# Three-pass matmul products over pairs of accumulators, and a third weight staging buffer, in a convolution and attention trunk step

## The chip, the cores and the metric

The kernel runs on one core of one Trainium2 chip. The metric is the device time of one execution in microseconds (us). In the shares and tables, PE is the matmul engine, PEld its weight loads, DVE the vector engine, ACT the scalar engine, POOL the GpSimd engine, and SP the engine that issues nearly all of the loads and stores.

## The reference

The reference computes one inference step of a trunk with two layers, D = 1024, in float32. The first layer is a convolution module and a SwiGLU feed-forward part (FFN). The second is chunked attention on one shared K/V and a second FFN. Cut to what this case touches:

```python
def swiglu_ffn(h, g, w_in, w_out):
    a, b = jnp.split(rms_norm(h, g) @ w_in, 2, axis=-1)
    return h + (jax.nn.silu(a) * b) @ w_out

def conv_module(h, hist, g, w_pw1, b_pw1, w_dw, b_dw, ln_g, ln_b, w_pw2, b_pw2):
    a, gate = jnp.split(rms_norm(h, g) @ w_pw1 + b_pw1, 2, axis=-1)
    glu = a * jax.nn.sigmoid(gate)
    full = jnp.concatenate([hist.astype(glu.dtype), glu], axis=1)
    y = lax.conv_general_dilated(full, w_dw[:, None, :], window_strides=(1,), padding="VALID", ...) + b_dw
    y = jax.nn.silu(layer_norm(y, ln_g, ln_b))
    return h + y @ w_pw2 + b_pw2, full[:, -CONV_HIST:]
```

There are 512 prompt tokens (one stream) and 128 sample tokens (8 streams of 16). The convolution is causal, one filter of width 31 for each channel. The FFN has 2816 hidden channels.

## The kernel before

**Data.** Activations lie with channels on the 128 partitions and tokens along the free axis, 8 channel tiles of 128. The 640 tokens are two groups: group 0 has 256 columns (the samples and the first prompt tokens), group 1 has 384.

**Products.** A float32 product is made of three products of rounded parts. Each operand is split into a high part, which is rounded, and a low part, the rest. `mm3` (L169) fills one accumulator in PSUM: for each of the 8 channel tiles k it issues high weights with high values (L172), low weights with high values (L173) and high weights with low values (L174), one behind the other. The pool `mm` has four accumulators.

**Weights.** `wsplit` (L130) brings a weight tile of 128 x 2048 into SBUF and splits it: SP loads `raw` (L141, or L136 for the second FFN product), ACT copies it to `whi` (L152), and `wlo = raw - whi` is made by DVE and POOL together (L156): POOL takes the last `pool` quarters of the columns, DVE the first ones. `raw`, `whi` and `wlo` have two buffers each in the pool `wp`. Such a tile serves two output tiles of 8 channel tiles, a first half and a second half.

**Stages.** The string `PLAN` sets in which order the early work is written; a scheduler, which runs on a timeline model, then sets the order in which each engine's queue holds it. In the convolution module `glu` (L371) multiplies with `in_w_pw` and gates; `conv` (L422) filters channel tiles on DVE, one instruction per filter tap into PSUM (L439); `conv_pool` filters others on ACT and POOL (L419); `conv_pe` filters others by matmuls (L471), whose operand goes from SBUF to DRAM (`sc`, L454) and back in shifted copies (`x`, L457). `conv_ln` (L476) makes the layer norm: sums of channel tiles on POOL (`acc`, L197), a matmul with ones (L206), one that spreads the result over the partitions (L218), y minus the mean, squares on ACT (L181) and their sums on POOL (L197), again L206 and L218, the product with the reciprocal deviation (L491), the activation (L493), and the split into high and low parts called z in the code and `x` in the profile (L161 on ACT, L162 on DVE). `pw2` (L498) multiplies z with the second pointwise weights: in group 1 two weight tiles at a time are in work. The FFN of group 0 (`ffn_in` L273, `out_tile` L298, `ffn_out` L307) is written between the convolution and the layer norm of group 1, so that PE has work while DVE filters group 1. In `ffn_in` each weight tile gives the two halves a and b of a hidden tile; silu(a)·b becomes `hid` (ACT L289, DVE L290), which is split as well (L161, L162). Behind `pw2` of group 1 stands the rest of the FFN, then attention, then the second FFN, whose matmuls are written elsewhere (L971).

Of the kernel before, what the change touches and what calls it, by code (L numbers as in the profile page):

```python
# [8 lines left out]
F32 = mybir.dt.float32  # L9
F32R = mybir.dt.float32r  # L10
AF = mybir.ActivationFunctionType
ALU = mybir.AluOpType
PSUM = bass.MemoryType.PSUM

P = 128
# [64 lines left out]
def tile_trunk(ctx, tc, xT, vecs, hist, w_pw1, w_pw2, w_in0, w_out0, w_in1, w_out1,  # L80
# [7 lines left out]

    uid = [0]
# [40 lines left out]
    def wsplit(src, k, n, parts=1, pool=0, cuts=1, gains=None):  # L130
        raw = wp.tile([P, 2048], F32, tag="raw", name=nm("raw"))
# [37 lines left out]
    def mm3(ps, wts, xs):  # L169
        last = len(wts) - 1  # L170
        for i, ((wh, wl), (xh, xl)) in enumerate(zip(wts, xs)):
            nc.tensor.matmul(ps, wh, xh, start=(i == 0), stop=False)  # L172
            nc.tensor.matmul(ps, wl, xh, start=False, stop=False)  # L173
            nc.tensor.matmul(ps, wh, xl, start=False, stop=(i == last))  # L174

# [97 lines left out]
    def ffn_in(wsrc, j, xs, hid, jj, groups, pool):  # L273
        wh, wl = wsplit(wsrc[j], 16, P, pool=pool)
        for g in groups:
            n = GR[g][1]
            ps = []
            for ab in range(2):
                pt = mmt()
                mm3(pt[:, :n], [(wh[:, (ab * 8 + k) * P:(ab * 8 + k + 1) * P],  # L280
                                 wl[:, (ab * 8 + k) * P:(ab * 8 + k + 1) * P]) for k in range(KT)],
                    xk(xs[g], range(KT)))
                ps.append(pt[:, :n])
# [14 lines left out]
    def out_tile(wts, ch, b, m, g, hid):  # L298
        wh, wl = wts
        n = GR[g][1]  # L300
        pt = mmt()
        mm3(pt[:, :n], [(wh[:, (b + k) * P:(b + k + 1) * P], wl[:, (b + k) * P:(b + k + 1) * P])
                        for k in range(ch)], xk(hid[g], range(ch)))
        with tc.high_priority(offset=HP):
            nc.vector.tensor_tensor(out=hp(g, m), in0=pt[:, :n], in1=hp(g, m), op=ALU.add)

    def ffn_out(wsrc, j0, ch, hid, groups, pool):  # L307
        mg = 4 if ch <= 4 else 2 if ch <= 8 else 1
        ws = []
        for m0 in range(0, KT, mg):  # L310
            src = wsrc[m0:m0 + mg, :, j0 * P:(j0 + ch) * P].rearrange("m p c -> p m c")
            ws.append(wsplit(src, ch * mg, P, parts=mg, pool=pool))
            if mg == 4:
                continue
            for m in range(m0, m0 + mg):
                for g in groups:
                    out_tile(ws[-1], ch, (m - m0) * ch, m, g, hid)
        if mg == 4:
            for g in groups:
                for m in range(KT):  # L320
                    out_tile(ws[m // mg], ch, (m % mg) * ch, m, g, hid)
# [49 lines left out]
    def glu(c, g, wh, wl):  # L371
        n = GR[g][1]
        ps = []
        for ab in range(2):
            pt = mmt()
            mm3(pt[:, :n], [(wh[:, (ab * 8 + k) * P:(ab * 8 + k + 1) * P],
                             wl[:, (ab * 8 + k) * P:(ab * 8 + k + 1) * P]) for k in range(KT)],
                xk(xs[g], range(KT)))
            ps.append(pt[:, :n])
# [118 lines left out]
    def pw2(g, z):  # L498
        n = GR[g][1]
        for m2 in range(KT // 2):  # L500
            wh, wl = wsplit(w_pw2[m2], 16, P, pool=PL2[g])
            for i in range(2):
                m = 2 * m2 + i
                pt = mmt()
                mm3(pt[:, :n], [(wh[:, (i * 8 + k) * P:(i * 8 + k + 1) * P],
                                 wl[:, (i * 8 + k) * P:(i * 8 + k + 1) * P]) for k in range(KT)],
                    xk(z, range(KT)))
                nc.vector.scalar_tensor_tensor(out=hp(g, m), in0=pt[:, :n], scalar=col(V_BPW2, m),
                                               in1=hp(g, m), op0=ALU.add, op1=ALU.add)
# [56 lines left out]
    hid0.close()  # L566

# [740 lines left out]
```

## Time and profile before

| | |
|---|---|
| time, median of 3 runs | 1544.46 us (1542.37 to 1546.8) |
| profiled execution: time | 1545.65 us |
| profiled execution: span | 1543.9 us |
| mean granted TensorE clock | 0.988 of full speed |
| instructions | 27207 |
| HBM read, written | 187.55 MB, 11.22 MB |
| matmul records of L172, L173, L174 from x (1344 each) | 412.5, 415.9, 411.9 us busy |
| the same from hid (352 each) | 104.4, 107.7, 105.9 us busy |
| whi (117 copies on ACT, L152) | 197.8 us busy, mean 1694 ns |

A row of a group of instructions gives the line, the engine, the operation, output and inputs by the program's names, the shapes, the count, then busy time and mean duration. A row of waits names who waited, "<-", for whom, then us in total, how often and the longest. A row of stretches gives start and end, the length, then for each engine its busy us (with its number of instructions), the granted clock, the share of the DMA engines and what they moved. A row of the timeline gives start, duration (of all merged instructions), the instruction, and in brackets the idle time before it and who ended it. The lines themselves stand in the prediction.

### The profile page before, as it was taken

Reading aid. Unit: us, or ns where it says so; the run is one execution under the profiler, and the core shown is the slowest. Engines: PE = TensorE matmul, PEld = TensorE weight load, DVE = VectorE, ACT = ScalarE, POOL = GpSimd, SP = SyncE. Lnnn points to the kernel's source line nnn. Section 1 sums busy time; section 2 is a strip of 40 time slices with the busy share of each in tenths; the row PEclk is TensorE's granted clock in tenths of the full one; section 3 lists DMA queues with packets and bytes.
Section 4 is the critical chain, followed back from the end, with each engine's and each line's share of the span. In section 5 each row is a group of like instructions: output and inputs, shape, how many; then the busy total and the mean of one; then the engine's idle time right before and its main releaser. Section 6 shows DMA issues by size and latency. Waiting matters only on the chain.

```text
span 1543.9 us, 27207 instructions
## 1 busy us (share of the span) xinstructions
PE 1470.9 (95%) x11054; PEld 1397.5 (91%) x11054; DVE 1041.2 (67%) x1890; ACT 666.6 (43%) x1196; POOL 450.6 (29%) x406
## 2 busy tenths in 40 slices
PE   5888998989999999999999999998999999999998
PEld 5878888988999999999988798886989999999998
DVE  6894999988545445456566767666797466467456
ACT  4544454535433323235455445443564144244244
POOL 6965468977501000001322111110421011011010
PEclk9999999999999999999999999998999999999999
DMA  7784335445421333433555545444003222222222
GB/s 232 240 228 143 138 113 164 144 156 164 137 83 56 130 116 130 133 118 124 194 180 196 182 143 200 150 153 140 28 28 116 76 83 89 76 83 89 76 83 83
DMA packets 57022, 200.54 MB, mean 130 GB/s; under 512 B 10176, under 2 KB 20672, under 8 KB 44096
## 3 DMA queue, kind: packets, MB, share of 16 engines
q1 hardware_dynamic: 56608, 198.48, 39.1%
q8 instruction: 87, 1.43, 0.4%
q10 hardware_dynamic: 288, 0.31, 0.1%
q14 instruction: 39, 0.32, 0.1%
HBM read 187.55 MB, written 11.22 MB: 129 GB/s over the span
## 4 chain that ended last, share of the span: by engine, by line
PE 71%; DVE 15%; DMA 4%; issue 4%; ACT 3%; POOL 3%; SPq 0%; POOLq 0%; ACTq 0%; DVEq 0%
PE mm L172 13%; PE mm L174 13%; PE mm L173 13%; PE pb L971 6%; DVE w L439 5%; PE pc L971 4%; PE pa L971 3%; DVE wlo L156 3%; PE w L797 1%; PE pb L172 1%; DMA raw<-in_w_pw 1%; PE pb L173 1%; PE pb L174 1%; PE pa L174 1%; PE pa L172 1%
## 5 line engine op out<-in xcount | busy, mean ns | idle before, releaser
L173 PE MATMUL mm<-x,wlo 128*128 128x256 f32 (+1 forms) x1344 | 415.9, 311 | 15.0 <-DVE wlo L156 14.1
L172 PE MATMUL mm<-x,whi 128*128 128x256 f32 (+1 forms) x1344 | 412.5, 311 | 6.1 <-ACT x L161 3.7
L174 PE MATMUL mm<-x,whi 128*128 128x256 f32 (+1 forms) x1344 | 411.9, 310 | 0.6 <-DVE x L162 0.3
L152 ACT ACTIVATE whi<-raw 128x2048 fp32r<-128x2048 f32 (+2 forms) x117 | 197.8, 1694 | 228.5 <-PE mm L174 138.0
L173 PEld LDWEIGHTS mm<-x,wlo 128*128 128x128 f32 x1344 | 255.7, 190 | 18.7 <-DVE wlo L156 17.0
L172 PEld LDWEIGHTS mm<-x,whi 128*128 128x128 f32 x1344 | 253.4, 190 | 11.3 <-ACT x L161 4.1
L174 PEld LDWEIGHTS mm<-x,whi 128*128 128x128 f32 x1344 | 254.0, 190 | 3.0 <-DVE x L162 1.9
L156 DVE TENSOR_TENSOR wlo<-raw,whi 128x2048 fp32r<-128x2048 f32 (+5 forms) x117 | 207.8, 1779 | 63.3 <-ACT whi L152 59.5
L156 POOL TENSOR_TENSOR wlo<-raw,whi 128x1536 fp32r<-128x1536 f32 (+3 forms) x50 | 146.5, 2932 | 66.8 <-ACT whi L152 66.5
L916 POOL TENSOR_TENSOR raw<-raw 128x512 f32<-128x512 f32 x38 | 56.4, 1485 | 327.0 <-DVE raw L916 262.9
L173 PE MATMUL mm<-hid,wlo 128*128 128x256 f32 (+1 forms) x352 | 107.7, 309 | 6.7 <-DVE wlo L156 6.7
L174 PE MATMUL mm<-hid,whi 128*128 128x256 f32 (+1 forms) x352 | 105.9, 307 | 0.8 <-DVE hid L162 0.7
L439 DVE SCALAR_TENSOR_TENSOR w<-gp,dwv,w 128x384 f32<-128x384 f32 x180 | 103.9, 612 | 0.8
L172 PE MATMUL mm<-hid,whi 128*128 128x256 f32 (+1 forms) x352 | 104.4, 307 | 0.0
L197 POOL TENSOR_TENSOR acc<-sq,sq 128x384 f32<-128x384 f32 (+1 forms) x8 | 8.0, 1004 | 259.6 <-ACT sq L181 259.5
L173 PEld LDWEIGHTS mm<-hid,wlo 128*128 128x128 f32 x352 | 66.1, 188 | 7.9 <-DVE wlo L156 7.9
L419 POOL TENSOR_TENSOR y<-y,cvt 128x256 f32<-128x256 f32 (+1 forms) x60 | 67.0, 1117 | 4.6 <-ACT cvt L418 2.2
L174 PEld LDWEIGHTS mm<-hid,whi 128*128 128x128 f32 x352 | 65.8, 188 | 1.2 <-DVE hid L162 1.2
L172 PEld LDWEIGHTS mm<-hid,whi 128*128 128x128 f32 x352 | 65.1, 188 | 0.2
L161 ACT ACTIVATE whi<-raw 128x1024 fp32r<-128x1024 f32 x38 | 39.4, 1054 | 54.7 <-DVE raw L916 19.1
L971 PE MATMUL pa<-x0f,whi 128*128 128x320 f32 x228 | 60.1, 311 | 2.7 <-DVE t L916 1.2
L197 POOL TENSOR_TENSOR acc<-acc,sq 128x384 f32<-128x384 f32 (+1 forms) x48 | 52.6, 1096 | 29.1 <-ACT sq L181 27.7
(326 smaller groups left out, 3496.6 us busy)
## 6 DMA issues: line engine op xcount, KB each, us to landing
raw<-in_w_in SPq DMA_DIRECT2D x62, 1024.0 KB
raw<-in_w_out SPq DMA_DIRECT2D x36, 768.0 KB
raw<-in_w_pw SPq DMA_DIRECT2D x22, 1024.0 KB
cache<-in_ck SPq DMA_DIRECT2D x32, 512.0 KB
cache<-in_cv SPq DMA_DIRECT2D x32, 512.0 KB
raw<-in_w_kq SPq DMA_DIRECT2D x8, 1024.0 KB
x<-sc SPq DMA_DIRECT2D x16, 368.0 KB
raw<-in_w_out SPq DMA_DIRECT2D x4, 1024.0 KB
```

Of the source, the lines that this page charges most:

```text
L152: nc.scalar.activation(out=hi[:, a:b], in_=raw[:, a:b], func=AF.Copy)
L156: eng.tensor_tensor(out=lo[:, a:b], in0=raw[:, a:b], in1=hi[:, a:b].bitcast(F32), op=ALU.subtract)
L161: nc.scalar.activation(out=hi, in_=src, func=AF.Copy)
L172: nc.tensor.matmul(ps, wh, xh, start=(i == 0), stop=False)
L173: nc.tensor.matmul(ps, wl, xh, start=False, stop=False)
L174: nc.tensor.matmul(ps, wh, xl, start=False, stop=(i == last))
L197: last["acc"] = eng.tensor_tensor(out=acc[:, :n], in0=prev, in1=s(), op=ALU.add)
L419: nc.gpsimd.tensor_tensor(out=y[g][:, c, :], in0=y[g][:, c, :], in1=pr[:, :n], op=ALU.add)
L439: nc.vector.scalar_tensor_tensor(out=dst, in0=src, scalar=wj, in1=dst, op0=ALU.mult, op1=ALU.add)
L797: nc.tensor.matmul(st[32 * b:32 * b + 32, 0:512], qv[b], KC[b // 2][:, b % 2, :], start=True, stop=True)
L916: ENG[e].tensor_tensor(out=out, in0=a, in1=b, op=op)
L971: nc.tensor.matmul(ps, a[:, c], b[:, k, :], start=(first and k == 0 and i == 0), stop=(k == 3 and i == 2), skip_group_check=not first)
```

## The change

A pool `rx` with one buffer is opened beside `wp`. Every third call of `wsplit` takes its `raw` from there, until the pool is closed ahead of attention; there are then three raw buffers in turn, while `whi` and `wlo` keep two each. A new function `mm3s` fills several accumulators together in three passes over all channel tiles: high with high, high weights with low values, low weights with high values; within a pass it goes through k, and at each k through the accumulators. `glu`, `ffn_in` and `pw2` give it the pair of output tiles of one weight tile, and `out_tile` becomes `out_tiles`, which takes pairs too (`ffn_out` then loops over groups outside the pair). Both accumulators of a pair are finished at its end, one matmul apart. The number of matmuls, vector, scalar and GpSimd instructions and loads stays what it was. Where attention and the second FFN use their own products, nothing is written anew, and PE's order there is unchanged.

```diff
+    rxs = ExitStack()
+    third = [0, rxs.enter_context(tc.tile_pool(name="rx", bufs=1, side="right"))]
...
     def wsplit(src, k, n, parts=1, pool=0, cuts=1, gains=None):
-        raw = wp.tile([P, 2048], F32, tag="raw", name=nm("raw"))
+        third[0] += 1
+        pool3, tag = (third[1], "rx") if third[1] and third[0] % 3 == 0 else (wp, "raw")
+        raw = pool3.tile([P, 2048], F32, tag=tag, name=nm(tag))
...
+    def mm3s(pss, wtss, xs):
+        n = len(xs) - 1
+        for step in range(3):
+            for i, (xh, xl) in enumerate(xs):
+                for ps, wts in zip(pss, wtss):
+                    wh, wl = wts[i]
+                    nc.tensor.matmul(ps, (wh, wh, wl)[step], (xh, xl, xh)[step],
+                                     start=(step == 0 and i == 0), stop=(step == 2 and i == n))
...
-            ps = []
-            for ab in range(2):
-                pt = mmt()
-                mm3(pt[:, :n], [(wh[:, (ab * 8 + k) * P:(ab * 8 + k + 1) * P],
-                                 wl[:, (ab * 8 + k) * P:(ab * 8 + k + 1) * P]) for k in range(KT)],
-                    xk(xs[g], range(KT)))
-                ps.append(pt[:, :n])
+            ps = [mmt()[:, :n] for _ in range(2)]
+            mm3s(ps, [[(wh[:, (ab * 8 + k) * P:(ab * 8 + k + 1) * P],
+                        wl[:, (ab * 8 + k) * P:(ab * 8 + k + 1) * P]) for k in range(KT)]
+                      for ab in range(2)], xk(xs[g], range(KT)))
...
-            for m in range(m0, m0 + mg):
-                for g in groups:
-                    out_tile(ws[-1], ch, (m - m0) * ch, m, g, hid)
+            for g in groups:
+                out_tiles(ws[-1], ch, range(0, mg * ch, ch), range(m0, m0 + mg), g, hid)
...
     ffn({1: hp1}, w_in0, w_out0, {1: xs1}, (1,), FD)
     hid1.close()
     hid0.close()
+    rxs.close()
+    third[1] = None
```

The scheduler sets the queues anew. The order is shown at three places; names end in the program's running number, which differs by a few between the two programs, and line numbers are 4 to 10 higher in the changed one.

**DVE, in the first FFN of group 0, beside the taps of group 1.** `t` is silu(a)·b of a hidden tile, `hid` its low part, `w_...` an accumulator of the taps in PSUM. Before:

```order
L290 TENSOR_TENSOR t_301_2409<-t_300_2408,mm_2383 128x256
L439 SCALAR_TENSOR_TENSOR w_366_2820<-gp,dwv,w_366_2820 128x384
L439 SCALAR_TENSOR_TENSOR w_367_2885<-gp,dwv,w_367_2885 128x384
L439 SCALAR_TENSOR_TENSOR w_366_2820<-gp,dwv,w_366_2820 128x384
L156 TENSOR_TENSOR wlo_2479<-raw_2477,whi_2478 128x512
L162 TENSOR_TENSOR hid_2161<-t_301_2409,hid_2161 128x256
```

Now:

```order
L160 TENSOR_TENSOR wlo_2482<-raw_2480,whi_2481 128x512
L447 SCALAR_TENSOR_TENSOR w_367_2888<-gp,dwv,w_367_2888 128x384
L300 TENSOR_TENSOR t_301_2412<-t_300_2411,mm_2362 128x256
L447 SCALAR_TENSOR_TENSOR w_366_2823<-gp,dwv,w_366_2823 128x384
L447 SCALAR_TENSOR_TENSOR w_367_2888<-gp,dwv,w_367_2888 128x384
L166 TENSOR_TENSOR hid_2164<-t_301_2412,hid_2164 128x256
```

The low weights have moved from a place behind t and three taps to a place ahead of t; t and hid have two taps between them where the low weights and three taps stood. Ahead of the last tap DVE holds 479 instructions before and 477 now.

**PE, the start of `pw2` in group 1.** `x_3013` (now `x_3016`) is z of group 1; an `Activation` wait is for a high part (of z, or of the weights), a `DVE` wait for a low part or for an accumulator. Before:

```order
L172 MATMUL mm_4195<-x_3013,whi_4189 128x384 [waits Activation_49]
L172 MATMUL mm_4221<-x_3013,whi_4189 128x384 [waits DVE_49]
L173 MATMUL mm_4195<-x_3013,wlo_4190 128x384 [waits DVE_49]
L174 MATMUL mm_4195<-x_3013,whi_4189 128x384
L172 MATMUL mm_4195<-x_3013,whi_4189 128x384
L173 MATMUL mm_4195<-x_3013,wlo_4190 128x384
```

Now:

```order
L186 MATMUL mm_4198<-x_3016,whi_4192 128x384 [waits DVE_49,Activation_49]
L186 MATMUL mm_4198<-x_3016,whi_4192 128x384 [waits Activation_49]
L186 MATMUL mm_4199<-x_3016,whi_4192 128x384 [waits DVE_49]
L186 MATMUL mm_4199<-x_3016,whi_4192 128x384
L186 MATMUL mm_4257<-x_3016,whi_4251 128x384 [waits DVE_49,Activation_49]
L186 MATMUL mm_4257<-x_3016,whi_4251 128x384
L186 MATMUL mm_4258<-x_3016,whi_4251 128x384 [waits DVE_49]
L186 MATMUL mm_4258<-x_3016,whi_4251 128x384
L186 MATMUL mm_4198<-x_3016,whi_4192 128x384 [waits Activation_49]
```

Before, the products of k stand in threes, and those of the last k come near the end of the 96 matmuls of the four accumulators. Now the 32 products of high parts of all four accumulators stand first, the last k of z from the 29th on, and then all with low values, and all with low weights.

**SP, the loads of the early convolution.** `raw` and `rx` are weight tiles of 1.0 MB; `sc` and `x` are the way through DRAM of `conv_pe`. Before:

```order
L141 DMA raw_599<-in_w_pw 128x2048
L141 DMA raw_666<-in_w_pw 128x2048
L454 DMA sc_735<-gs 128x740
L141 DMA raw_883<-in_w_pw 128x2048
L457 DMA x_94_737<-sc_735 32x4x736 x4
L141 DMA raw_950<-in_w_pw 128x2048
L454 DMA sc_778<-gs 128x740
L141 DMA raw_1045<-in_w_pw 128x2048
L457 DMA x_98_780<-sc_778 32x4x736 x4
L141 DMA raw_1158<-in_w_pw 128x2048
L543 DMA out_convs<-gs 1024x1x368
L454 DMA sc_1108<-gs 128x740
```

Now:

```order
L145 DMA raw_669<-in_w_pw 128x2048
L145 DMA raw_886<-in_w_pw 128x2048
L145 DMA rx_953<-in_w_pw 128x2048
L462 DMA sc_738<-gs 128x740
L465 DMA x_94_740<-sc_738 32x4x736 x4
L145 DMA raw_1048<-in_w_pw 128x2048
L145 DMA raw_1161<-in_w_pw 128x2048
L462 DMA sc_781<-gs 128x740
L145 DMA rx_1447<-in_w_pw 128x2048
L465 DMA x_98_783<-sc_781 32x4x736 x4
L145 DMA raw_1509<-in_w_pw 128x2048
L551 DMA out_convs<-gs 1024x1x368
```

One or two more weight tiles now stand ahead of each `sc`: `raw_886` and `rx_953` ahead of the first, and `rx_1447` and `raw_1509` ahead of the third, which followed it before.

More of the change, by code (lines that the diff above doesn't have):

```diff
@@ L296, in ffn_in, with out_tiles @@
                 xsplit(t[:, :n], hid[g][0][:, jj, :], hid[g][1][:, jj, :])
-    def out_tile(wts, ch, b, m, g, hid):
+    def out_tiles(wts, ch, bs, ms, g, hid):
         wh, wl = wts
         n = GR[g][1]
[L301 to L305, printed above, removed]
+        ps = [mmt()[:, :n] for _ in ms]
+        mm3s(ps, [[(wh[:, (b + k) * P:(b + k + 1) * P], wl[:, (b + k) * P:(b + k + 1) * P])
+                   for k in range(ch)] for b in bs], xk(hid[g], range(ch)))
+        for m, pt in zip(ms, ps):
+            with tc.high_priority(offset=HP):
+                nc.vector.tensor_tensor(out=hp(g, m), in0=pt, in1=hp(g, m), op=ALU.add)
     def ffn_out(wsrc, j0, ch, hid, groups, pool):
@@ L314, in ffn_out @@
                 continue
-            for m in range(m0, m0 + mg):
-                for g in groups:
-                    out_tile(ws[-1], ch, (m - m0) * ch, m, g, hid)
+            for g in groups:
+                out_tiles(ws[-1], ch, range(0, mg * ch, ch), range(m0, m0 + mg), g, hid)
         if mg == 4:
             for g in groups:
-                for m in range(KT):
-                    out_tile(ws[m // mg], ch, (m % mg) * ch, m, g, hid)
+                for m in range(0, KT, 2):
+                    out_tiles(ws[m // mg], ch, ((m % mg) * ch, (m % mg + 1) * ch), (m, m + 1), g,
+                              hid)
     def ffn(pool, w_in, w_out, xs, groups, chunks, pl=0, og=None, cm=CM, pad=(0, 0)):
@@ L372, in glu @@
         n = GR[g][1]
[L373 to L379, printed above, removed]
+        ps = [mmt()[:, :n] for _ in range(2)]
+        mm3s(ps, [[(wh[:, (ab * 8 + k) * P:(ab * 8 + k + 1) * P],
+                    wl[:, (ab * 8 + k) * P:(ab * 8 + k + 1) * P]) for k in range(KT)]
+                  for ab in range(2)], xk(xs[g], range(KT)))
         with tc.high_priority(offset=HP):
@@ L501, in pw2 @@
             wh, wl = wsplit(w_pw2[m2], 16, P, pool=PL2[g])
-            for i in range(2):
-                m = 2 * m2 + i
[L504 to L508, printed above, removed]
+            ps = [mmt()[:, :n] for _ in range(2)]
+            mm3s(ps, [[(wh[:, (i * 8 + k) * P:(i * 8 + k + 1) * P],
+                        wl[:, (i * 8 + k) * P:(i * 8 + k + 1) * P]) for k in range(KT)]
+                      for i in range(2)], xk(z, range(KT)))
+            for i, pt in enumerate(ps):
+                m = 2 * m2 + i
+                nc.vector.scalar_tensor_tensor(out=hp(g, m), in0=pt, scalar=col(V_BPW2, m),
                                                in1=hp(g, m), op0=ALU.add, op1=ALU.add)
```

## The prediction

> **What bounds the kernel now.** I read the page first, then all engines by stretches of the span.
>
> ```profile
> PE 1470.9 (95%) x11054; PEld 1397.5 (91%) x11054; DVE 1041.2 (67%) x1890; ACT 666.6 (43%) x1196; POOL 450.6 (29%) x406
> ...
> 80.00:120.00 40.00, 34.68 (x290) 28.54 (x292) 35.50 (x71) 16.90 (x27) 21.84 (x21) 0.91 0.83 236
> 150.00:200.00 50.00, 44.91 (x341) 40.43 (x342) 48.71 (x80) 24.25 (x37) 24.19 (x14) 0.93 0.37 129
> 200.00:250.00 50.00, 45.06 (x359) 43.13 (x358) 50.00 (x88) 27.32 (x42) 38.95 (x20) 1.00 0.37 115
> 250.00:300.00 50.00, 44.75 (x373) 43.55 (x374) 50.00 (x84) 26.69 (x34) 45.34 (x23) 1.00 0.51 173
> 395.00:450.00 55.00, 55.00 (x357) 55.00 (x356) 27.67 (x43) 21.88 (x33) 17.29 (x10) 1.00 0.33 114
> 600.00:720.00 120.00, 120.00 (x694) 120.00 (x694) 62.14 (x73) 40.02 (x44) 2.26 (x3) 1.00 0.37 123
> ```
>
> PE is busy for 95% of the span. It has no idle time at all from 395 on, where the first FFN of group 1 runs (the last two rows are the two ends of it). So what the change gives must come from ahead of 395. There the limit differs. From 150 to 300 DVE is full (48.71, 50.00 and 50.00 of 50 us), while PE has some 5 us idle in each 50: PE waits for what DVE makes. Now the waits of PE: first the whole span, then 150 to 300, then 300 to 400.
>
> ```profile
> PE mm L173 <- DVE wlo L156: 20.8, 18, 3.6
> PE mm L471 <- DMA x<-sc: 8.4, 2, 4.6
> ...
> PE mm L172 <- ACT whi L152: 1.2, 2, 1.0
> ...
> PE mm L173 <- DVE wlo L156: 11.5, 13, 2.4
> ...
> PE mm L173 <- DVE wlo L156: 9.3, 5, 3.6
> ```
>
> The three passes aim at the wait for low weights. It is 20.8 us in all, 11.5 of it where DVE is full and 9.3 behind that. These are the most that the edit can take away directly.
>
> **The change, part by part. Matmuls.** Their number and shapes stay. New is that PE changes its accumulator at every matmul.
>
> ```profile
> 288.98 0.28 PE L172 MATMUL mm<-x,whi 128*128 128x256 f32 x1
> 289.10 0.28 PE L173 MATMUL mm<-x,wlo 128*128 128x256 f32 x1
> ...
> 598.78 0.34 PE L173 MATMUL mm<-x,wlo 128*128 128x384 f32 x1
> 598.95 0.34 PE L174 MATMUL mm<-x,whi 128*128 128x384 f32 x1
> ...
> 1250.73 0.31 PE L971 MATMUL pa<-x0f,whi 128*128 128x320 f32 x1
> 1250.88 1.92 PE L971 MATMUL pb<-xe,bk 128*128 128x320 f32 x12
> ```
>
> Starts are 0.12 us apart with 256 columns and 0.17 with 384. In the second FFN a change from accumulator `pa` to `pb` costs no more than its 320 columns, 0.15. I take the alternation at nothing. Bounds: a hundredth either way of the some 720 us where it is used would be 7 us, but the rows give no reason for either sign.
>
> **Stretch 0 to 154.** Two tiles wait there for their high weights (1.2 us in the waits above), which an earlier load can take away. Against that, one or two more weight tiles stand on SP ahead of the convolution's way through DRAM. Its worst case now is on the chain:
>
> ```profile
> 81.08 9.73 DMA sc<-gs
> ...
> 102.58 6.49 PE L471 MATMUL mm<-x,w 128*32 128x256 f32 x64 [4.64 <-DMA x<-sc]
> ```
>
> A tile of 1.05 MB at the 236 GB/s of the row 80 to 120 is 4.4 us. Queued ahead of `sc` it delays that matmul by up to this; the PE work moved in front can win back as much. Bounds −4.4 and +4.4 (for the first of the two loads the same tiles were already nearly through), I take −0.5.
>
> **Stretch 150 to 338.** Here DVE sets the pace, and the change takes nothing from it: as many low weights, taps and splits stand ahead of the last tap (477 instructions for 479). PE now asks for the low weights only at its 33rd matmul of a tile, 32 x 0.12 = 3.8 us later. That hides a wait of 0.3 to 2.4 us once; but a PE that runs ahead of a full DVE waits for the next thing it makes (`hid`, a freed accumulator). So of the 11.5 us I count nothing for the last tap. What DVE's own instructions cost is open:
>
> ```profile
> L439 DVE SCALAR_TENSOR_TENSOR w<-gp,dwv,w 128x384 f32<-128x384 f32 x180 | 103.9, 612 | 0.8
> L156 DVE TENSOR_TENSOR wlo<-raw,whi 128x512 fp32r<-128x512 f32 x13 | 23.5, 1806 | 0.0
> ...
> L162 DVE TENSOR_TENSOR hid<-t,hid 128x256 fp32r<-128x256 f32 x12 | 10.0, 833 | 0.0
> ...
> 322.81 3.56 DVE L156 TENSOR_TENSOR wlo<-raw,whi 128x512 fp32r<-128x512 f32 x1
> 335.67 0.69 DVE L156 TENSOR_TENSOR wlo<-raw,whi 128x512 fp32r<-128x512 f32 x1 [1.51 <-ACT whi L152]
> 336.27 3.71 DVE L162 TENSOR_TENSOR hid<-t,hid 128x256 fp32r<-128x256 f32 x1
> ...
> 335.71 3.99 POOL L156 TENSOR_TENSOR wlo<-raw,whi 128x1536 fp32r<-128x1536 f32 x1 [2.42 <-ACT whi L152]
> ```
>
> (The first three rows are the groups of 154 to 328.) The same 512 columns took 0.69 us and 3.56; the `hid` of 256 columns took 3.71 while POOL's share of the low weights ran from 335.71 to 339.70, and ended as that ended. The taps, whose long operand lies in PSUM and not in SBUF, keep to 0.6. So a DVE instruction with both inputs in SBUF can be held up by POOL's. The changed order sets low weights, t and hid differently against POOL's part; the mean of 1.81 may go to 0.69 or to 3.56. I take no change, and price the two sides as rivals below. The Trainium skill, page "SBUF — State Buffer", section "Who interferes with whom", states this as a rule: such an instruction shares a read port with GpSimd, and who issues first blocks the other for the whole instruction; by that rule the cost hangs on who comes first, which the new order may settle either way. The rows agree (3.71 beside POOL's 3.99, 0.69 just ahead of it).
>
> **Layer norm of group 1.**
>
> ```profile
> 327.15 1.26 DVE L439 SCALAR_TENSOR_TENSOR w<-gp,dwv,w 128x384 f32<-128x384 f32 x2
> ...
> 329.65 3.64 POOL L197 TENSOR_TENSOR acc<-acc,y 128x384 f32<-128x384 f32 x3
> ...
> 307.57 0.38 PE L173 MATMUL mm<-hid,wlo 128*128 128x256 f32 x1 [1.38 <-DVE wlo L156]
> 313.95 0.39 PE L173 MATMUL mm<-hid,wlo 128*128 128x256 f32 x1 [1.68 <-DVE wlo L156]
> 326.42 0.39 PE L173 MATMUL mm<-x,wlo 128*128 128x256 f32 x1 [3.56 <-DVE wlo L156]
> 338.65 0.72 PE L206 MATMUL w<-onec,acc 128*128 128x1 f32 x6
> ...
> 324.00:328.00 4.00, 1.58 (x9) 1.58 (x10) 3.96 (x5) 0.80 (x1) 4.00 (x2) 0.85 0.23 31
> 328.00:332.00 4.00, 4.00 (x27) 4.00 (x27) 2.24 (x2) 1.25 (x3) 3.92 (x3) 0.72 0.81 264
> ```
>
> The last tap ends at 328.4, POOL's sums at 333.3, yet PE's L206 that reads them comes at 338.65: here PE is late by 5.4 us, since 1.38 + 1.68 + 3.56 = 6.6 us of waits lie ahead, and behind the longest of them the granted clock was 0.85 and 0.72 (0.15 x 1.6 + 0.28 x 4 = 1.4 us). If these 8.0 us go, and PE still has 24 matmuls more ahead of L206 than before (24 x 0.12 = 2.9), L206 comes 5.1 us earlier, just behind the sums. Bounds 0 and 5.4; I take 4, as PE then waits more for DVE. The Trainium skill, page "TensorE: Matmul & The Clock Gate", section "HAM oscillation — how this bites in real kernels", puts the limit at a gap of some 3.4 us, behind which the clock halves; by it the term for the clock would be half of 3.4, 1.7 us in place of 1.4. The trace agrees: the gap of 3.56 was followed by 0.72.
>
> **`pw2` of group 1** takes part of this back.
>
> ```profile
> 368.97 0.72 PE L206 MATMUL w<-onec,acc 128*128 128x1 f32 x6
> ...
> 381.24 6.54 DMA raw<-in_w_pw
> ...
> 389.83 1.23 DVE L156 TENSOR_TENSOR wlo<-raw,whi 128x1024 fp32r<-128x1024 f32 x1 [2.05 <-ACT whi L152]
> ...
> 394.98 0.92 ACT L161 ACTIVATE x<-n 128x384 fp32r<-128x384 f32 x2
> ...
> 403.15 0.51 PE L172 MATMUL mm<-x,whi 128*128 128x384 f32 x2
> ```
>
> L206 at 368.97 follows POOL's second sums, so the 4 us hold up to z. The load of 6.54 us, on the chain now, starts sooner through the third buffer, which also takes DVE's idle 2.05 us for its low weights away. The last high part of z, at 394.98 + 0.92 = 395.9 now, so comes at 395.9 − 4 − 2.05 = 389.8. But the three passes need all eight high parts within the first 32 of the 96 matmuls of four accumulators: behind the last part stand 4 + 64 = 68 matmuls, 68 x 0.173 = 11.8 us, so they end at 401.6. Before they end at about 403.2, as the last part was needed only near the end (403.15 is the first row behind them). Gain 1.6 us; with 5.4 for 4 it is 3.0; with nothing saved ahead of z the last part comes at 393.9 and they end at 405.7, 2.5 later than now. I take a gain of 2.5: ACT too gives z's last parts sooner when its copies of weights no longer fall between them.
>
> **From 395 on** nothing: PE is full and its order from attention on is the old one. The waits for low weights that the passes would hide there are none: the row from 395 to 450 has 55.00 of 55.
>
> **The sum** against the profiled execution: 1545.65 − 0.5 − 2.5 = 1542.65. That execution lies 1.2 above the median of 1544.46, so the forecast is 1.8 under the median. About 0.3%, 4.6 us, is what a measurement tells from no change: 1539.8 to 1549.1 count as same.
>
> **Rivals.** (B) *The waits really go and DVE gets faster.* If the low weights' 13 instructions of 512 columns fall from 1.81 us to near the 0.69, DVE's stretch is shorter by up to 13 x 1.1 = 14.5 us, and the last tap with it. For it: DVE is full there, and each us passes to the last tap. Against: the same two engines split the same tiles at the same signal, whi. With two thirds of it, 9.7, and the sum's 3.0: 1533; with all of the 14.5, 1528.
>
> (C) *Slower: DVE is held up more.* Place: DVE's low weights and `hid` in 150 to 328. Price: the 12 rows of `hid` at a mean of 0.83 us reach 3.71 when they fall into POOL's 3.99; the hid split now stands some 2.5 us (wlo, tap, t, two taps) behind the low weights that start with POOL's part, so still within it. If a third of the 12 is hit more, 4 x 2.9 = 11.5 us later, less the sum's 3: 1545.65 + 11.5 − 3 = 1554; with a quarter 1551. It decides from a hold-up of 1549.1 − 1542.65 = 6.5 us on, where the time leaves the same.
>
> (D) *The loads behind more weight tiles.* The two waits of 8.4 us on `x<-sc` grow by up to 4.4: 1542.65 + 4.9 = 1547.5. For: SP is one queue, and the row 80 to 120 has the DMA engines 83% busy. Against: the extra tile is wanted anyway, and its later place is then free.
>
> (E) *The change does not do what it says:* with two buffers for whi and wlo still, a third raw tile only waits longer for its split, and z's end eats what the passes win. Then 1545.65.
>
> **How the numbers follow.** Forecast 0.47, of which 0.10 falls under 1539.8 and 0.37 within same (its own range 1538 to 1547); B 0.25, all faster; C 0.15, slower; D 0.08, of which 0.02 slower; E 0.05, same. Faster 0.10 + 0.25 = 0.35; same 0.37 + 0.06 + 0.05 = 0.48; slower 0.15 + 0.02 = 0.17. The range leaves out about a third of B at the bottom and of C at the top: 1530 to 1552.
>
> **What would show it.** Right: PE's wait for low weights falls from 20.8 to under 3, but DVE stays full from 150 to 300 and the last tap stays within 3 us of 328.4; PE's L206 comes at 333 to 336 in place of 338.65; PE then waits inside the first 32 matmuls of `pw2` for high parts of z; from there on both traces run in parallel, some 3 us apart. Wrong: a last tap at 318 or earlier (B) or at 333 and later (C), with the mean of low weights on DVE moved from 1.81; a wait on `x<-sc` above 8.4 in all (D); or a pitch other than 0.12 and 0.17 in dense stretches.

## The result, and the profile after

| | median | range | runs |
|---|---|---|---|
| before | 1545.39 us | 1542.37 to 1546.80 | 4 |
| changed | 1568.65 us | 1567.57 to 1569.97 | 4 |

The changed kernel is slower: ratio 1.0158, 95% interval 1.0140 to 1.0177. The profiled execution of the changed kernel has a span of 1565.9 us (1543.9 before), 22.0 more. First its engines and its stretches (the same cuts as before, columns as in the table of before), then what PE waits for over the whole span, and at last PE's waits from 0 to 150 alone.

```profile
PE 1481.7 (95%) x11054; PEld 1409.6 (90%) x11054; DVE 1045.9 (67%) x1890; ACT 668.8 (43%) x1196; POOL 448.4 (29%) x406
...
80.00:120.00 40.00, 34.98 (x270) 29.42 (x268) 33.88 (x69) 17.11 (x29) 24.24 (x23) 0.91 0.78 221
150.00:200.00 50.00, 42.28 (x320) 38.08 (x318) 45.91 (x74) 24.25 (x36) 25.62 (x16) 0.86 0.32 107
200.00:250.00 50.00, 40.58 (x293) 38.67 (x290) 49.29 (x74) 23.51 (x37) 28.01 (x16) 0.93 0.33 96
250.00:300.00 50.00, 43.61 (x336) 42.81 (x335) 49.06 (x79) 22.25 (x28) 41.12 (x22) 0.90 0.47 158
300.00:340.00 40.00, 33.34 (x260) 32.54 (x259) 37.40 (x61) 17.75 (x25) 30.19 (x17) 0.91 0.36 110
395.00:450.00 55.00, 51.27 (x317) 50.86 (x317) 32.74 (x48) 27.28 (x38) 22.18 (x13) 0.94 0.43 149
500.00:600.00 100.00, 100.00 (x608) 99.98 (x607) 50.84 (x69) 32.42 (x42) 6.06 (x8) 1.00 0.32 107
```

```profile
PE mm L186 <- DVE t L300: 16.5, 9, 2.4
PE mm L186 <- ACT x L165: 11.7, 8, 3.3
PE mm L479 <- ACT t L393: 5.4, 2, 4.8
PE mm L479 <- DMA x<-sc: 4.7, 1, 4.7
PE w L231 <- POOL rst L245: 3.9, 2, 2.7
PE mm L186 <- DVE h L316: 3.7, 1, 3.7
...
PE mm L186 <- DVE wlo L160: 0.2, 1, 0.2
...
PE mm L186 <- ACT x L165: 2.7, 3, 1.5
```

The reader is to see three things. The wait for low weights, 20.8 us before, is down to 0.2: the change does what it is built for. In its place stand 16.5 us for `t` (silu(a)·b, whose making frees the second accumulator of a pair) and 11.7 us for high parts of x. And PE, with the same 11054 matmuls, is busy for 1481.7 us where it was 1470.9: idle time makes 84.2 − 73.0 = 11.2 of the 22.0 us, and slower matmuls the other 10.8, as the granted clock of 150 to 340 shows (0.86 to 0.93; before 0.93 to 1.00).

When the same work is reached in the two profiled executions, in us from the span's start:

| place | before | changed | later by |
|---|---|---|---|
| second sums of group 0's layer norm (PE L206, ahead of z) | 148.8 | 152.9 | 4.1 |
| first high part of x of group 0, for the FFN (ACT) | 197.4 | 206.0 | 8.6 |
| last one, end | 205.8 | 219.9 | 14.1 |
| t of the first hidden tile (DVE) | 215.1 | 231.7 | 16.6 |
| t of the sixth | 246.2 | 263.8 | 17.6 |
| last tap, end | 328.4 | 347.0 | 18.6 |
| first sums of group 1's layer norm (PE L206) | 338.65 | 358.02 | 19.4 |
| first sum h of `pw2` in group 1 (DVE) | 398.5 | 419.0 | 20.5 |
| last sum of the first FFN | 730.4 | 754.3 | 23.9 |

So nearly all is lost by the last tap, and the largest piece, 12.5 of it, between 153 and 232. Of these 12.5 us 4.5 are lost up to the first high part of x, while `pw2` of group 0 is multiplied (the granted clock of 150 to 200 is 0.86, 0.93 before), and 8.0 behind it, where x of group 0 is normalised and the first two hidden tiles are multiplied. Here is that second part in the timeline of the changed kernel, DVE, POOL, ACT and PE one behind the other:

```profile
195.34 3.42 DVE L160 TENSOR_TENSOR wlo<-rx,whi 128x512 fp32r<-128x512 f32 x1
211.84 3.14 DVE L166 TENSOR_TENSOR x<-n,x 128x256 fp32r<-128x256 f32 x1
215.77 0.68 DVE L160 TENSOR_TENSOR wlo<-raw,whi 128x512 fp32r<-128x512 f32 x1
...
194.72 3.49 POOL L160 TENSOR_TENSOR wlo<-rx,whi 128x1536 fp32r<-128x1536 f32 x1 [2.35 <-PE mm L186]
211.23 3.47 POOL L160 TENSOR_TENSOR wlo<-raw,whi 128x1536 fp32r<-128x1536 f32 x1 [10.84 <-ACT whi L156]
...
219.49 0.40 ACT L165 ACTIVATE x<-n 128x256 fp32r<-128x256 f32 x1
...
217.34 1.22 PE L186 MATMUL mm<-x,whi 128*128 128x256 f32 x4 [3.33 <-ACT x L165]
219.95 5.17 PE L186 MATMUL mm<-x,whi 128*128 128x256 f32 x31 [1.39 <-ACT x L165]
```

One low part of x, 0.42 us elsewhere, takes 3.14 while POOL splits the weights of the second hidden tile, and that tile's `wlo` of DVE stands in the queue ahead of the last two parts of x. PE stops for the seventh and for the eighth high part, as its first pass asks for all of them.

### The profile page after: what moved, and what is told of

The parts are those of the page before. It is cut to its first block, busy times and chain, and to the rows that moved or that the text cites. A ratio compares the mean times of both kernels' runs of the same rounds, so it can differ in the third digit from the quotient of the medians.

```text
span 1565.9 us, 27254 instructions
## 1 busy us (share of the span) xinstructions
PE 1481.7 (95%) x11054; PEld 1409.6 (90%) x11054; DVE 1045.9 (67%) x1890; ACT 668.8 (43%) x1196; POOL 448.4 (29%) x406
## 4 chain that ended last, share of the span: by engine, by line
PE 70%; DVE 13%; ACT 3%; issue 2%; POOL 1%; DMA 1%; POOLq 0%; DVEq 0%; ACTq 0%
PE mm L186 25%; PE pb L981 6%; PE mm L176 4%; PE pc L981 4%; PE mm L177 4%; PE mm L178 4%; DVE wlo L160 4%; PE pa L981 4%; DVE w L447 3%; ACT whi L156 1%; PE pb L176 1%; PE pb L177 1%; PE pb L178 1%; PE w L807 1%; PE pa L178 1%
## 5 line engine op out<-in xcount | busy, mean ns | idle before, releaser
L186 PE MATMUL mm<-x,whi 128*128 128x384 f32 (+1 forms) x2176 | 347.5, 317 | 25.7 <-ACT x L165 11.7
L186 PEld LDWEIGHTS mm<-x,whi 128*128 128x128 f32 x2176 | 332.9, 196 | 32.3 <-ACT x L165 13.8
L156 ACT ACTIVATE whi<-raw 128x2048 fp32r<-128x2048 f32 (+2 forms) x87 | 143.7, 1657 | 158.3 <-PE mm L186 94.4
L186 PE MATMUL mm<-x,wlo 128*128 128x384 f32 (+1 forms) x1088 | 169.9, 308 | 0.2 <-DVE wlo L160 0.2
L186 PEld LDWEIGHTS mm<-x,wlo 128*128 128x128 f32 x1088 | 161.0, 188 | 0.3 <-DVE wlo L160 0.3
L186 PE MATMUL mm<-hid,whi 128*128 128x256 f32 (+1 forms) x704 | 113.7, 316 | 8.4 <-DVE t L300 6.3
L186 PEld LDWEIGHTS mm<-hid,whi 128*128 128x128 f32 x704 | 107.4, 196 | 10.3 <-DVE t L300 6.9
L160 POOL TENSOR_TENSOR wlo<-raw,whi 128x1536 fp32r<-128x1536 f32 (+3 forms) x33 | 89.8, 2726 | 64.5 <-ACT whi L156 45.6
L176 PE MATMUL mm<-x,whi 128*128 128x256 f32 (+1 forms) x256 | 80.5, 315 | 1.1 <-DVE h L316 1.1
L177 PE MATMUL mm<-x,wlo 128*128 128x256 f32 (+1 forms) x256 | 79.9, 312 | 0.0
L178 PE MATMUL mm<-x,whi 128*128 128x256 f32 (+1 forms) x256 | 79.5, 310 | 0.0
L160 DVE TENSOR_TENSOR wlo<-rx,whi 128x2048 fp32r<-128x2048 f32 (+4 forms) x30 | 60.2, 2006 | 9.2 <-ACT whi L156 9.2
```

The costliest lines, as they stand in the source:

```text
L156: nc.scalar.activation(out=hi[:, a:b], in_=raw[:, a:b], func=AF.Copy)
L160: eng.tensor_tensor(out=lo[:, a:b], in0=raw[:, a:b], in1=hi[:, a:b].bitcast(F32), op=ALU.subtract)
L186: nc.tensor.matmul(ps, (wh, wh, wl)[step], (xh, xl, xh)[step], start=(step == 0 and i == 0), stop=(step == 2 and i == n))
```

## The experiments

Each kernel was run beside the kernel before on the same chip; a ratio is to that kernel, with its 95% interval. Times in us are medians.

### Which half of the change

Third buffer alone (`wsplit` as in the change, `mm3` as before):

```diff
-        raw = wp.tile([P, 2048], F32, tag="raw", name=nm("raw"))
+        third[0] += 1
+        pool3, tag = (third[1], "rx") if third[1] and third[0] % 3 == 0 else (wp, "raw")
+        raw = pool3.tile([P, 2048], F32, tag=tag, name=nm(tag))
```

> The third staging buffer alone, products as before the change. Theory R (the third buffer puts weight tiles ahead of the convolution's loads, and that is what the 23 us are): about 1555 to 1568 us, and the waits on x<-sc above the 8.4 us of before. Theory X (the first pass needs all eight high parts of x at once) and theory P (both accumulators of a pair must be free at its first matmuls, and are released only at its end): within 5 us of before, 1540 to 1550, with some 20 us of waits for low weights as before.

Measured: 1541.37, ratio 0.9979 (0.9966 to 0.9992). Three passes alone, two raw buffers:

```diff
-    third = [0, rxs.enter_context(tc.tile_pool(name="rx", bufs=1, side="right"))]
+    third = [0, None]
```

> The three passes over pairs as in the change, but two staging buffers as before it. R: near the time before, 1545 to 1552. X and P: nearly all of the loss stays, 1561 to 1570, with waits of PE for the high parts of x and for t (silu(a)*b, which frees the second accumulator) of 10 us and more each.

Measured: 1571.12, ratio 1.0162 (1.0128 to 1.0196). So the third buffer is not the cause, and all of the loss comes with the passes over pairs. Without the third buffer the waits on `x<-sc` were 15.0 us, so the delay of the early convolution is not owed to it either: the scheduler sets SP's queue anew for every variant. The 0.2% of the third buffer alone are not located: at the last sum of the first FFN that profiled execution is 1.3 us behind the one before, and its gain lies behind that, in attention and the second FFN, which the buffer doesn't touch.

### What in the passes: the pair, or the order within it

One accumulator after the other, each in three passes:

```diff
-        for step in range(3):
-            for i, (xh, xl) in enumerate(xs):
-                for ps, wts in zip(pss, wtss):
+        for ps, wts in zip(pss, wtss):
+            for step in range(3):
+                for i, (xh, xl) in enumerate(xs):
```

> As the change, but the three passes run over one accumulator, then over the other of the pair; so the first is released half a tile earlier, and the second is needed half a tile later. P: the waits for t fall from 16.5 us to under 4 and the time by some 8 to 14 us, to 1555 to 1561. X: the high parts of x are needed even sooner (8 matmuls), those waits stay at 10 us or more, and the time stays at 1563 to 1570.

Measured: 1560.59, ratio 1.0101 (1.0071 to 1.0131). The waits for t fell to 5.1 us, near what theory P expected, though 16.3 us of waits on `x<-sc` came up. Pairs, but by channel tile:

```diff
-        for step in range(3):
-            for i, (xh, xl) in enumerate(xs):
+        for i, (xh, xl) in enumerate(xs):
+            for step in (0, 2, 1):
```

> As the change, but within a pair all three products of a channel tile k stand together, so that high parts of x are needed one by one as before the change; both accumulators are still filled together. X: the waits for high parts of x fall from 11.7 us to under 4, and the time by 8 to 14 us, to 1555 to 1561. P: the waits for t stay near 16 us and the time at 1563 to 1570. Waits for low weights come back under both, as they are needed at the third matmul or so.

Measured: 1549.76, ratio 1.0024 (1.0008 to 1.0039), better than theory X expected. PE's waits in this kernel:

```profile
PE mm L186 <- DVE wlo L160: 23.1, 19, 3.8
PE w L219 <- DVE acc L210: 12.8, 1, 12.8
PE mm L186 <- ACT x L165: 6.3, 2, 5.3
...
PE mm L176 <- DVE h L316: 2.5, 1, 2.5
```

The pairs are still there, but the waits for `t` of a hidden tile are gone from the list and the old wait for low weights is back, 23.1 us of it, and the kernel is 19 us faster than the changed one. So theory P as I put it falls too: a pair held to its end does not by itself make PE wait for t; only with low weights out of the way does PE come early enough for that. The pairs do cost something, 0.45% against the third buffer alone (1.0024 and 0.9979, with intervals that don't overlap). The larger piece, 1.34% between 1.0024 and 1.0158, hangs on the order of the products within the pair. A milder form of the passes, one accumulator at a time, with the low weights behind all the rest:

```diff
+    def mm3w(ps, wts, xs):
+        last = len(wts) - 1
+        for i, ((wh, wl), (xh, xl)) in enumerate(zip(wts, xs)):
+            nc.tensor.matmul(ps, wh, xh, start=(i == 0), stop=False)
+            nc.tensor.matmul(ps, wh, xl, start=False, stop=False)
+        for i, ((wh, wl), (xh, xl)) in enumerate(zip(wts, xs)):
+            nc.tensor.matmul(ps, wl, xh, start=False, stop=(i == last))
```

> Third staging buffer, one accumulator at a time as before the change, and two passes: for each channel tile high with high and high weights with low values, then all low weights. High parts of x are asked for one by one (every second matmul), accumulators are released as before, and low weights are needed 16 matmuls (1.9 us) later than before. If the loss of the change comes from asking for all high parts at once and from the pair (theories X and P), this keeps the gain without the loss: 1533 to 1545 us, waits for low weights under 8 us. If any delay of the low-weight products shifts the queues to the same loss (theory S, the scheduler sets DVE's and SP's queues in another order), 1555 to 1568.

Measured: 1554.12, ratio 1.0064 (1.0042 to 1.0086): a miss for X and P, which don't apply to it, and between the expectations. Its waits for low weights fell to 4.9 us, others took their place:

```profile
PE mm L483 <- ACT cvt L430: 9.5, 1, 9.5
PE mm L483 <- DMA x<-sc: 8.0, 2, 7.2
PE mm L183 <- ACT x L165: 6.4, 4, 2.7
PE mm L184 <- DVE hid L166: 5.7, 5, 2.4
PE mm L184 <- DVE x L166: 5.4, 5, 2.0
PE mm L186 <- DVE wlo L160: 4.9, 8, 1.2
```

The rows on `hid` and x (5.7 and 5.4 us; 0.7 and 0.3 before) say the same as those of the changed kernel: whoever no longer waits for low weights waits for the next thing that DVE makes. The two longest, 9.5 us for `cvt` on ACT and 8.0 on `x<-sc`, lie ahead of 150, in the early convolution, where the scheduler has set the queues anew.

### Where in the program

Three passes in the FFN alone, and in `glu` and `pw2` alone; the other part by channel tile, in pairs (`mm3k` is the function of the pairs by channel tile above):

```diff
-        mm3s(ps, [[(wh[:, (ab * 8 + k) * P:(ab * 8 + k + 1) * P],
+        mm3k(ps, [[(wh[:, (ab * 8 + k) * P:(ab * 8 + k + 1) * P],
```

> As the change (third buffer, pairs), but three passes only in the FFN (ffn_in, out_tiles); in glu and pw2 the three products of a channel tile stand together. If the loss sits in the FFN beside the taps (x of the freshly normalised group 0, pairs held to their end): 1558 to 1567. If it sits in the early convolution and in pw2: 1545 to 1552. The last run, pairs by channel tile everywhere, had 1549.8.

> The other half of the change: three passes over pairs only in glu and pw2, pairs by channel tile in the FFN, third buffer. With passes in the FFN alone the loss was 10.5 us. If the two halves add up to the change's 23: 1556 to 1560. If each half alone brings about the same shift of the queues: the same 1554 to 1558. If glu and pw2 cost nothing: 1546 to 1552.

Measured: 1556.21, ratio 1.0079 (1.0055 to 1.0103), and 1557.63, ratio 1.0083 (1.0053 to 1.0112). The first lies between its two expectations, the second within two of its three (the halves add up, or each half brings about the same shift). From the 1.0024 of pairs by channel tile everywhere, the halves add 0.55% and 0.59%; the sum, 1.0138, comes near the change's 1.0158, so they add up within the intervals, and no single stage owns the loss.

### Collisions of DVE and GpSimd

GpSimd's share of the split left out, in the changed kernel and in the kernel before:

```diff
-                        eng.tensor_tensor(out=lo[:, a:b], in0=raw[:, a:b],
-                                          in1=hi[:, a:b].bitcast(F32), op=ALU.subtract)
+                if c < b:
+                    nc.gpsimd.memset(lo[:, c:b].bitcast(F32), 0.0)
```

> The changed kernel, but GpSimd's share of each split into low weights is left out; a fill with zeros, which reads nothing from SBUF, stands in its place. To be compared with the same edit in the kernel before. Theory C (DVE is held up by GpSimd's reads in other places than before, worth some 6 of the 18.6 us by which the last tap is late): the distance between the two falls from 23 us to 14 to 19. Theory X, P or S without C: the distance stays at 20 to 26. If collisions are all of it: under 6.

> The kernel before with the same part left out (GpSimd's share of the split into low weights, filled with zeros). DVE's low weights of 512 columns should take about 0.7 us each, where they took 1.8; the last tap then comes some 20 to 25 us sooner (12 of hid, 25 of low weights), and the time falls to 1515 to 1530 if nothing else binds.

Measured: 1515.26 (ratio 0.9806, 0.9785 to 0.9826) and 1509.77 (0.9774, 0.9748 to 0.9801). The distance falls from 23 us to 5.5, under the 6 that I had set for collisions as the whole cause. A row of DVE of the second, then PE by stretches of the first:

```profile
L155 DVE TENSOR_TENSOR wlo<-raw,whi 128x512 fp32r<-128x512 f32 x14 | 10.5, 747 | 4.7 <-ACT whi L152 2.6 <-issue 2.1
...
200.00:250.00 50.00, 48.29 (x421) 48.09 (x421) 49.12 (x96) 38.09 (x59) 42.36 (x39) 1.00 0.50 158
250.00:300.00 50.00, 50.00 (x443) 50.00 (x442) 48.63 (x98) 22.62 (x25) 17.98 (x15) 1.00 0.61 205
```

512 columns of `wlo` take 747 ns where they took 1806, so the price of sharing with GpSimd was real. The last tap comes at 307.0 (before's order) and 304.9 (the change's): with DVE relieved, the three passes even reach it first. This edit takes work off GpSimd as well as reads, so it doesn't show that collisions are all of it. The next was meant to separate the two: DVE splits alone in the FFN of group 0, nothing is left out.

```diff
-PFA = 3
-PFB = 3
+PFA = 0
+PFB = 0
```

> The kernel before, but in the FFN of group 0 (beside the taps) DVE splits the whole weight tile and GpSimd takes no share; nothing is left out. Theory C (collisions of DVE with GpSimd's reads): a split of 2048 columns takes 2.3 us on DVE where the 512 columns beside GpSimd took 1.8, hid falls from 9 to 5 us in all, so DVE's work to the last tap grows by some 8 us only; GpSimd's sums of the layer norm of group 1 are free of the splits among them. 1530 to 1545 us. If collisions were not the cost and the share only work moved to a full engine: 14 x 1.2 + 8 x 0.9 = 24 us more on DVE, 1555 to 1570.

> The changed kernel with the same: in the FFN of group 0 DVE splits alone. C: the distance to the run before this one is under 8 us (it was 23 with GpSimd's share). X and P (high parts all at once, pairs held to their end), which do not need a collision: the distance stays at 18 or more.

> Third staging buffer with products as before the change, and DVE splits alone in the FFN of group 0. The third buffer alone gave 0.2%; if that adds up: 3 us under the first run of this group. As a version: below 1541, the best whole kernel so far, if C holds.

Measured: 1565.5 (ratio 1.0130, 1.0102 to 1.0159) for the kernel before, 1570.12 (1.0154, 1.0119 to 1.0189) for the changed one, 1563.7 (1.0122, 1.0090 to 1.0154) with the third buffer alone. The distance is again small, 4.6 us, but the level is 20 us up: for the kernel before, the share that GpSimd takes is worth more than its collisions cost, a miss for what I expected of a version without it. And the small distance is not clean evidence for collisions: both kernels wait here for the layer norm's sums on POOL (13.4 us and 22.9 us of PE's waits), behind last taps at 369.6 and 380.9, which are 41 and 34 us later than with GpSimd's share, so they share a bound that hides the difference. The last tap of the changed kernel is still 11.3 us behind the other's, of 18.6 with GpSimd's share: without GpSimd's part of these splits a good part of the delay is still there.

### At the place of the largest piece

The high weights last, so that their buffer is held to the pair's end:

```diff
-                    nc.tensor.matmul(ps, (wh, wh, wl)[step], (xh, xl, xh)[step],
+                    nc.tensor.matmul(ps, (wh, wl, wh)[step], (xh, xh, xl)[step],
```

> The change with its passes in another order: high with high, low weights with high values, high weights with low values. High weights are now read to the pair's end, as before the change; low weights are needed 16 matmuls into the pair. All eight high parts of x are still asked for in the first pass, and pairs are held to their end. Theory S (the early release of the high weights' buffer puts the next split among the parts of x, and into GpSimd's way): the last high part of x of group 0 comes within 10 us of the first, as before (it was 13.4), and the time falls to 1550 to 1560. X and P: 1564 to 1570.

Measured: 1569.04, ratio 1.0157 (1.0136 to 1.0179): nothing gained at the end. But the first half of theory S came true. DVE's queue holds the second hidden tile's `wlo` behind x again, the high parts of x come within 8.3 us of each other (205.0 to 213.3; 8.3 before, 13.9 in the change), and the last tap ends at 334.2 in place of 347.0:

```profile
330.96 3.24 DVE L447 SCALAR_TENSOR_TENSOR w<-gp,dwv,w 128x384 f32<-128x384 f32 x5
...
338.90 0.72 PE L219 MATMUL w<-onec,acc 128*128 128x1 f32 x6
...
150.00:200.00 50.00, 41.67 (x306) 38.71 (x304) 45.76 (x75) 25.70 (x37) 24.78 (x19) 0.86 0.38 127
200.00:250.00 50.00, 47.25 (x378) 44.06 (x374) 49.96 (x85) 25.61 (x42) 35.75 (x18) 1.00 0.38 114
250.00:300.00 50.00, 41.23 (x324) 39.50 (x323) 49.36 (x76) 22.43 (x27) 40.50 (x22) 0.97 0.47 155
```

From 150 to 200 and from 250 to 300 PE loses as much as in the change or more (41.67 and 41.23 busy of 50 us; 42.28 and 43.61 there), and only between the two less (47.25; 40.58). From 340 to 395 it loses again: it is busy for 47.5 of the 55 us, where it was for 51.4 before and 52.9 in the change. So L206 of group 1 (the code's L219 here) comes at 338.90, as early as before the change, but the first sum of `pw2` at 411.5 (398.5 before, 419.0 in the change), and the last sum of the first FFN at the change's 754. A last tap that is nearly in time doesn't give the time back while PE is behind with its own work.

The first two hidden tiles split by DVE alone; their products by channel tile; and both:

```diff
-                ffn_in(w_in, j0 + jj, xs, hid, jj, groups, pl)
+                ffn_in(w_in, j0 + jj, xs, hid, jj, groups, pl if j0 + jj > 1 else 0)
...
-            mm3s(ps, [[(wh[:, (ab * 8 + k) * P:(ab * 8 + k + 1) * P],
+            (mm3s if j > 1 or groups != (0,) else mm3k)(ps, [[(wh[:, (ab * 8 + k) * P:(ab * 8 + k + 1) * P],
```

> The change, with the first two weight tiles of the FFN split by DVE alone, so that GpSimd reads nothing while x of group 0 is made. C (the collision there): the 3.14 us of one low part of x fall to 0.42, t of the first hidden tile comes 3 to 6 us sooner and the time falls to 1561 to 1565. S or X without the collision: 1566 to 1571, since DVE has 1.6 us more of each split.

> The change, with the products of the first two weight tiles of the FFN by channel tile, still in pairs: x of group 0 is asked for part by part. X: PE's waits for high parts of x fall from 11.7 us by 5 or more and the time to 1556 to 1563. S and C: x itself is as late as in the change, and the time stays at 1565 to 1570.

> Both edits in the first two tiles: DVE splits alone, products by channel tile. If both collision and the asking for all parts hold at this place, the gains add: 1552 to 1560; if neither, 1565 to 1570.

Measured: 1559.18 (ratio 1.0093, 1.0076 to 1.0110), 1565.01 (1.0116, 1.0083 to 1.0149), 1562.47 (1.0114, 1.0099 to 1.0129). With GpSimd away from the two tiles the low part of x that took 3.14 us takes 0.42, t of the first hidden tile comes 7.4 us sooner (3 to 6 was expected), and 0.65% of the 1.58% are won back, somewhat more than expected. So GpSimd's share of these two tiles is a part of the cause, by the collision that the rows show there; that nothing else in the new queues helps isn't shown. Asking for x part by part in the same two tiles wins less, 0.42%, with overlapping intervals; waits for x fell from 11.7 to 6.1 us, waits for t stayed at 15.4, and the time is at the lower end of what theories S and C expected. Both together win no more than one, a miss (1552 to 1560 if the gains add): t of the first tile is then only 3.4 us behind the kernel before, and by the third it is 10.3 behind. What was won at the first tile was lost in the next two.

| kernel | ratio | PE busy, idle us (profiled) | PE's waits for wlo, x, t |
|---|---|---|---|
| before | 1 | 1470.9, 73.0 | 20.8, 3.7, – |
| changed | 1.0158 | 1481.7, 84.2 | 0.2, 11.7, 16.5 |
| third alone | 0.9979 | 1467.7, 71.7 | 20.8, 6.9, – |
| pairs by channel tile, third | 1.0024 | 1470.1, 77.1 | 23.1, 6.3, – |
| low weights last, third | 1.0064 | 1470.1, 81.0 | 4.9, 6.4, – |
| high weights last | 1.0157 | 1481.2, 86.7 | 10.6, 12.5, 6.8 |
| first two tiles by DVE | 1.0093 | 1478.8, 79.7 | –, 12.4, 13.5 |

(A dash: not among the waits listed.)

## Why the prediction was wrong

The forecast was 1542.65 us, with 1530 to 1552 as its range; 1568.65 were measured. The forecast also has a slip in itself: it takes 3.0 us off the profiled execution, which lies 1.2 us above the median, so for the median it should have been 1541.5.

**What bounds the kernel** was read rightly ahead of 395: DVE stayed near full from 150 to 300. PE is full from 500 to 600 as before (100.00 of 100 us). "From 395 on nothing" did not quite hold: between the first sum of `pw2` and the last sum of the first FFN another 3.4 us are lost, which the runs do not locate, and 1.9 are won back behind that. And "no idle time at all from 395 on" is true of the kernel before up to 720 only: from 740 to 1115 its PE was busy for 368.18 of 375 us.

**The waits for low weights** fell as forecast, to 0.2 us, under the 3 that I gave.

**The matmuls' pitch** stayed at 0.173 us in the dense stretch and 0.118 in the FFN of group 0; the alternation costs nothing.

**Stretch 0 to 154**: −0.5 taken, +4.1 measured, inside the bounds of ±4.4. The waits on `x<-sc` fell from 8.4 to 4.7 us, but 5.4 us on `t` of `glu` came up beside them, 2.7 on x (1.0 before), and the clock of 40 to 80 was 0.91 for 0.96.

**Stretch 150 to 338 is the step that failed**: "So of the 11.5 us I count nothing for the last tap" and "I take no change" for DVE's own instructions. I bounded what PE could win by hiding waits, and took it that a PE stalled by something else stalls no longer than before. The runs show that it did, in three ways. From the second sums of group 0's layer norm to the last tap the stretch took 14.5 us more (194.1 for 179.6): 8.6 of them in DVE's instructions, and 5.9 in DVE's idle time (7.8 us for 1.9). Summed without overlaps, low weights took 51.7 us for 43.2 (25 of them for 26), x 8.5 for 5.4, `hid` 5.4 for 9.0, taps 101.7 for 100.4. PE's waits from 150 to 338 became fewer and longer: 17 of together 30.1 us, for 20 of 22.6. And behind them its clock fell: over the whole span PE's busy time grew by 10.8 us at the same matmuls, where I had counted the clock only as a gain of 1.4.

**Rival C** named the right engines and the right place, and its signs came: a last tap behind 333 (347.0) and a changed mean of the low weights. But its time of 1551 to 1554 is still 15 us short, and it had the wrong victim: `hid`, which was to be hit, was relieved, since the low weights now stand ahead of t in DVE's queue and take the collision themselves. That its price of 11.5 us lies near the 14.5 of the stretch is luck in part: low weights, x and `hid` together took a net 8.0 more, and most of the rest is DVE's idle time, which C did not have. The Trainium skill's page "SBUF — State Buffer", section "Who interferes with whom", has two SBUF inputs on DVE contend with GpSimd's reads, who issues first blocking the other; the rows agree: 3.14 us for the low part of x that began 0.6 us behind POOL's split of 3.47, 747 ns in place of 1806 when GpSimd reads nothing. The order of a queue therefore decides what a collision hits, and I had the order before me for one place only.

**Rivals B and E.** B had DVE's low weights get cheaper; they got dearer. Here are the two groups of 512 columns in the changed kernel, 150 to 348 (2360 and 2447 ns, for 1806):

```profile
L160 DVE TENSOR_TENSOR wlo<-raw,whi 128x512 fp32r<-128x512 f32 x9 | 21.2, 2360 | 0.4 <-ACT whi L156 0.4
L160 DVE TENSOR_TENSOR wlo<-rx,whi 128x512 fp32r<-128x512 f32 x5 | 12.2, 2447 | 0.0
```

E had the change not do its work; it did, and that was not enough.

**L206 of group 1** was forecast at 333 to 336; it came at 358.0, behind the late last tap. **`pw2`** was to stall in its first 32 matmuls for z. It stalls there, but for an accumulator: behind the fourth matmul PE waits 3.7 us until DVE's `h` of L316 frees one (the row stands among the waits above). Behind that the clock is lower (0.94 for 395 to 450, 1.00 before), and it finds all parts of z in time, the last of which ends at 411.6. So of the sum's gain of 2.5 us nothing came: the delay grows from 18.6 us at the last tap to 20.5 at the first sum of `pw2`.

What is shown: the loss does not come with the third buffer; of the 1.79% between the third buffer alone and the change, 0.45 come with pairs by channel tile and 1.34 with the order of the passes; most of it is gone when GpSimd's share of the split is left out, which relieves GpSimd of work too; taking GpSimd out of the first two hidden tiles alone gives back 0.65 of the 1.58%. What stays open is how the rest divides between collisions further on, x asked for all at once and the backlog of PE: every variant also gets other queues from the scheduler, and of the edits that leave nothing out and keep the three passes over pairs in all stages none gave back more than that 0.65%. Whether the passes would pay with the old queues of DVE and SP wasn't tried.

## What to carry to other kernels

A wait is worth its length only if the engine waited for has something to spare: where DVE is full, a PE that no longer stalls for low weights stalls for x and for accumulators instead, in fewer and longer pieces. Before an order is changed so that an operand is needed later, list what is then needed sooner (here all eight high parts of x and both accumulators) and see whether the same full engine makes it. And look at how the change moves that engine's own queue: a low part of x of 0.42 us that landed beside GpSimd's reads took 3.14 here.

## What the runs showed of the hardware

The granted clock fell behind gaps shorter than I had taken as safe. Before, gaps of 2.12 and 2.42 us (at 212 and 266) left it at 1.00. In the changed kernel, these are PE's timeline at two gaps and the 4-us stretches around them (the clock is the third number from the end):

```profile
252.55 3.81 PE L186 MATMUL mm<-x,whi 128*128 128x256 f32 x20 [1.82 <-DVE t L300]
...
293.66 3.66 PE L186 MATMUL mm<-x,whi 128*128 128x256 f32 x19 [2.14 <-DVE t L300]
...
252.00:256.00 4.00, 3.45 (x20) 3.45 (x21) 4.00 (x10) 2.57 (x4) 2.09 (x2) 0.70 0.62 197
292.00:296.00 4.00, 2.34 (x14) 2.34 (x15) 4.00 (x9) 2.36 (x3) 1.66 (x3) 0.82 0.53 176
296.00:300.00 4.00, 4.00 (x29) 4.00 (x28) 4.00 (x6) 0.63 (x2) 4.00 (x2) 0.75 0.23 94
```

Gaps of 1.82 and 2.14 us are followed by 0.70, and by 0.82 and 0.75. The Trainium skill, page "TensorE: Matmul & The Clock Gate", section "HAM oscillation — how this bites in real kernels", names idle gaps of over some 3.4 us; here shorter ones did it, though not each time (1.42 at 237.6 and 1.78 at 244.8 left it at 1.00). The gap's length alone does not say whether the clock falls.
